# 15 of the 31 taps of a convolution's second half move from VectorE to GpSimd

## The chip, the cores and the metric

The kernel runs on one core of a Trainium2 chip. The metric is the device time of one launch in microseconds (us). The engines are called as in the profile: PE is TensorE, DVE is VectorE, ACT is ScalarE, POOL is GpSimd, SP is SyncE. An instruction is named by its line in the kernel, as L436.

## The reference, cut to what matters

One decoder layer works on 512 prompt tokens and 8 x 4 sample tokens, 1024 features wide. Its token mixer has three branches on the same input; the third is a convolution module: a gated product, a causal depthwise convolution of width 31 over 256 channels, a layer norm, a swish and a matrix.

```python
glu = c_in[..., :W_CONV] * jax.nn.sigmoid(c_in[..., W_CONV:])
cc, new_conv = _dwconv(glu, conv_buf, conv_dw, conv_b)
br_c = jax.nn.silu(_layernorm(cc, conv_ln_g, conv_ln_b)) @ conv_pw
merged = gates[:, :, 0] * br_a + gates[:, :, 1] * br_b + gates[:, :, 2] * br_c
```

`_dwconv` gives, for each channel and token t, the sum over j from 0 to 30 of weight[j] times glu[t - 30 + j], plus a bias. All is in 32-bit floats.

## The kernel before, in words

Features lie on the 128 partitions, tokens along the columns, so the 256 channels of the convolution are two blocks c = 0 and 1 of 128 partitions. `ge[c]` holds the gated product of a block with its 30 tokens of history, `acc[c]` the convolved result: 32 sample columns, then 512 prompt columns.

The matrix products are made by `gemm` (L228), each from three passes over operands split into a high and a low part. The high part of a weight chunk is written by ACT (L133), the rest by DVE (L134); the chunk can be used when both are there.

The convolution is in `conv_work`, a generator. For the sample tokens POOL forms products (L425, 128x248) and DVE sums them (L426, L427). For the prompt tokens DVE does one tap after the other: the first is a multiplication with the bias added (L434), each further one is L436, which multiplies a shifted view of `ge[c]` by a column of weights and adds `acc[c]`, on 128x512. The two blocks alternate. That makes two L434 and 60 L436. With `NV1 = 31` the branch that would use ACT and POOL for block 1 is never taken. `conv_norm` then transposes `acc` on PE (L457), normalises it and makes the operands that the sample stage multiplies much later.

Which instruction stands where in an engine's queue is not the order of the code. A planner lays the queues out by its own estimate of durations, following data dependences and giving preference to what comes earlier in the code. On the chip each queue then runs in that order. The code reaches the convolution (`pump(100)`) after the first attention unit, yet its taps stand in the DVE queue from 44 us on, between other work: the weight parts L134, the gate products L499, the parts of queries and keys L218 and L215, and L515. L515 scales the products of the pooling branch out of the "z" buffer in PSUM; there is one such buffer (a pair of banks), and the next product into it (L511, later L581) needs it empty. Half of these read-outs are done by ACT (L517), half by DVE (L515), eight each.

POOL's queue in this stage holds copies of state (L357, L384, L401, L405), the products L425, and the issue of a few DMAs (L385, L386, L406, L407); later it copies keys (L546) and issues the gathers of the cache.

Of the kernel before, what the change touches and what calls it, by code (L numbers as in the profile page):

```python
# [9 lines left out]
F32 = mybir.dt.float32  # L10
# [3 lines left out]
ALU = mybir.AluOpType  # L14
PSUM = bass.MemoryType.PSUM

P = 128
D = 1024
KD = D // P
NP = 512  # L20
DB = 8
DS = 4
NS = DB * DS
T = NP + NS
# [7 lines left out]
CW = 31  # L32
# [15 lines left out]
V_BG, V_PS, V_CB, V_CG, V_CLB, V_G1, V_B1, V_DW, V_SB, V_SR = 0, 24, 32, 34, 36, 38, 46, 54, 116, 124  # L48
# [5 lines left out]
NGA = 2  # L54
NGB = 3
PUMP = 4
NV1 = 31
GACT = 3
VACT = False
CNU = 0  # L60
# [88 lines left out]
def hybrid_layer_kernel(  # L149
# [6 lines left out]
    nc = tc.nc  # L156
# [79 lines left out]
    def vcol(c):  # L236
        return vt[:, c:c + 1]

    def sview(ap, s):
        return ap.rearrange("p (b s) -> p b s", s=s)  # L240
# [32 lines left out]
    cvp = conv_st.enter_context(pool("cvp"))  # L273
    GEW = CB + NP + DB * CEXT
    ge = [cvp.tile([P, GEW], F32, tag="ge", bufs=2, name=f"ge{c}") for c in range(2)]
    acc = [cvp.tile([P, T], F32, name=f"acc{c}") for c in range(2)]
# [76 lines left out]
    for c in range(2):  # L353
# [11 lines left out]
        for lev in range(2 if c == 0 else 4):  # L365
            sh = 1 << lev
            a0 = 2 * sh - 1
            o = s1.tile([P, n], F32, tag=f"sum{lev}", name=f"sum{c}{lev}")
# [5 lines left out]
        for s in range(2):  # L374
            r = slice(64 * s, 64 * s + 64)
            nc.vector.scalar_tensor_tensor(out=pf[r, NS + PB:], in0=sm[s][r, 2 * PB:PB + NP], scalar=ec_(E_IW + c, 1)[r],
                                           in1=ue[r, 2 * PB:PB + NP], op0=ALU.mult, op1=ALU.subtract)
            nc.vector.scalar_tensor_tensor(out=sview(pf[r, :NS], DS), in0=sview(sm[s][r, PB + NP:], PEXT)[:, :, PB:], scalar=ec_(E_IW + c, 1)[r],
                                           in1=uv[r, :, PB:], op0=ALU.mult, op1=ALU.subtract)
# [38 lines left out]
    def conv_work():  # L418
        for c in range(2):
            gv = sview(ge[c][:, CB + NP:], CEXT)  # L420
            dw = vt[:, V_DW + c * CW:V_DW + (c + 1) * CW].unsqueeze(1).to_broadcast([P, DB, CW])
            pr = cvp.tile([P, DS, DB, CW], F32, tag="prs", name=f"prs{c}")
            av_ = sview(acc[c][:, :NS], DS)
            for s in range(DS):
                nc.gpsimd.tensor_tensor(out=pr[:, s], in0=gv[:, :, s:s + CW], in1=dw, op=ALU.mult)  # L425
            nc.vector.reduce_sum(av_.rearrange("p b s -> p s b"), pr, axis=mybir.AxisListType.X)  # L426
            nc.vector.tensor_scalar(acc[c][:, :NS], acc[c][:, :NS], vcol(V_CB + c), None, op0=ALU.add)  # L427
            yield
        for j in range(CW):
            for c in range(2):  # L430
                dw = vcol(V_DW + c * CW + j)
                o, v = acc[c][:, NS:], ge[c][:, j:j + NP]
                if j == 0:
                    nc.vector.tensor_scalar(o, v, dw, vcol(V_CB + c), op0=ALU.mult, op1=ALU.add)  # L434
                elif c == 0 or j < NV1:
                    nc.vector.scalar_tensor_tensor(out=o, in0=v, scalar=dw, in1=o, op0=ALU.mult, op1=ALU.add)  # L436
                else:
                    pr = cvp.tile([P, NP], F32, tag="pr", bufs=2, name=f"pr{j}", padded_shape=[P, T])
                    nc.scalar.mul(pr, v, dw)
                    nc.gpsimd.tensor_tensor(out=o, in0=pr, in1=o, op=ALU.add)  # L440
            yield

    def conv_norm():
        rows = (P, P, P, P, NS)
# [29 lines left out]
        return last  # L474

    cw = conv_work()

    def pump(n):
# [615 lines left out]
    for m in range(KD):  # L1094
# [10 lines left out]
        for (c0, c1), ps in zip(HALVES, pss):  # L1105
            v = xf[:, m, c0:c1]
# [183 lines left out]
```

## Time and profile before

| | |
|---|---|
| time, median of 3 runs | 866.68 us (865.34 to 867.08) |
| time of the profiled execution | 872.77 us |
| its span | 871.0 us |
| PE busy | 827.4 us (95%), 6683 instructions |
| DVE busy | 580.5 us (67%), 968 instructions |
| ACT busy | 413.4 us (47%), 711 instructions |
| POOL busy | 174.1 us (20%), 198 instructions |
| mean granted TensorE clock | 0.975 |

The busy shares are means over stages that differ: the page's picture of the span in 40 slices has DVE at 8 or 9 tenths from the second to the fifth slice, 22 to 109 us, and at 4 to 6 tenths in many others. An instruction's duration includes time in which it is held up after its start; neighbouring instructions on DVE overlap by a little (a fill of some 0.07 us), so their number over the time they take together gives a somewhat smaller figure than their mean duration. The releaser in brackets is the instruction that ended the idle time before a row, as the profile infers it.

### The profile page before, as it was taken

The numbers are of one execution on the slowest core, as the hardware profiler recorded it, in microseconds if no ns is written. First come the engines' busy times: TensorE is split into PE (matmuls) and PEld (weight loads), VectorE is DVE, ScalarE is ACT, GpSimd is POOL, SyncE is SP. The second block draws the span as 40 slices with busy tenths as digits, with TensorE's granted clock in tenths as the row PEclk, the third lists the DMA queues.
The fourth block names the chain that finished last, engine by engine and source line by source line (L and its number), as shares of the span: only waits on it lengthen the run. The fifth ranks groups of instructions, "written<-read, shape, count | busy, mean of one in ns | idle before, by whom it ended". The sixth has DMA issues, their size and how long they took to land.

```text
span 871.0 us, 16214 instructions
## 1 busy us (share of the span) xinstructions
PE 827.4 (95%) x6683; PEld 779.1 (89%) x6683; DVE 580.5 (67%) x968; ACT 413.4 (47%) x711; POOL 174.1 (20%) x198
## 2 busy tenths in 40 slices
PE   8998899999999998999998699999999999999992
PEld 7998799888898786789997699999999999999992
DVE  4899956888555544469455999883337888843436
ACT  5334368677654324344316556553124555543231
POOL 1430000002547766210000032211000111110002
PEclk9999899999999998999999699999999999999997
DMA  9413132412738987673500153322225333312222
GB/s 297 125 48 106 55 93 62 147 40 87 266 119 289 341 320 259 216 272 116 146 2 1 48 145 99 97 68 82 85 83 146 98 98 100 108 55 83 74 93 103
DMA packets 119401, 110.35 MB, mean 127 GB/s; under 512 B 4896, under 2 KB 111232, under 8 KB 117152
## 3 DMA queue, kind: packets, MB, share of 16 engines
q1 hardware_dynamic: 110848, 73.12, 28.2%
q0 software_dynamic: 8480, 36.20, 11.9%
q8 instruction: 52, 0.85, 0.4%
q14 instruction: 21, 0.17, 0.1%
HBM read 104.44 MB, written 4.87 MB: 125 GB/s over the span
## 4 chain that ended last, share of the span: by engine, by line
PE 81%; DVE 8%; DMA 5%; issue 2%; ACT 2%; POOL 1%; SPq 0%; DVEq 0%; POOLq 0%; ACTq 0%
PE mm L228 73%; DVE acc L436 3%; DMA raw<-in_w_in 2%; PE z L581 1%; PE o L607 1%; DVE wl L134 1%; PE tp L602 1%; PE z L677 1%; PE o L704 1%; PE tp L819 1%; DMA vr<-in_cv,piv 1%; DMA kr<-in_ck,pix 1%; DMA xt<-in_x_t 1%; ACT wh L133 0%; ACT xf L897 0%
## 5 line engine op out<-in xcount | busy, mean ns | idle before, releaser
L228 PE MATMUL mm<-xh,wh 128*128 128x256 f32 (+1 forms) x672 | 198.3, 295 | 3.0 <-DVE gt L492 0.9
L228 PE MATMUL mm<-xl,wh 128*128 128x256 f32 (+1 forms) x672 | 196.8, 293 | 0.5 <-DVE xl L215 0.4
L228 PE MATMUL mm<-xh,wl 128*128 128x288 f32 (+1 forms) x672 | 196.4, 293 | 0.4 <-DVE wl L134 0.4
L133 ACT CAST wh<-raw 128x1024 fp32r<-128x1024 f32 (+2 forms) x93 | 84.8, 915 | 164.0 <-PE mm L228 142.8
L134 DVE TENSOR_TENSOR wl<-raw,wh 128x1024 fp32r<-128x1024 f32 (+2 forms) x93 | 100.1, 1079 | 71.5 <-ACT wh L133 70.9
L228 PEld LDWEIGHTS mm<-xh,wh 128*128 128x128 f32 x672 | 128.0, 191 | 9.2 <-issue 3.8
L228 PEld LDWEIGHTS mm<-xl,wh 128*128 128x128 f32 x672 | 127.8, 190 | 4.5 <-issue 3.1
L228 PEld LDWEIGHTS mm<-xh,wl 128*128 128x128 f32 x672 | 127.8, 191 | 3.5 <-issue 2.4
L228 PE MATMUL mm<-gh,wh 128*128 128x288 f32 (+1 forms) x352 | 101.6, 290 | 0.0
L228 PE MATMUL mm<-gh,wl 128*128 128x288 f32 (+1 forms) x352 | 101.3, 288 | 0.0
L228 PE MATMUL mm<-gl,wh 128*128 128x288 f32 (+1 forms) x352 | 100.8, 287 | 0.0
L644 POOL DMA_INDIRECT kr<-in_ck,pix x64 | 67.0, 1047 | 36.1 <-issue 14.8
L228 PEld LDWEIGHTS mm<-gl,wh 128*128 128x128 f32 x352 | 66.4, 189 | 0.0
L228 PEld LDWEIGHTS mm<-gh,wl 128*128 128x128 f32 x352 | 66.2, 188 | 0.0
L228 PEld LDWEIGHTS mm<-gh,wh 128*128 128x128 f32 x352 | 65.9, 188 | 0.1
L978 POOL TENSOR_TENSOR gl<-g,gh 128x272 fp32r<-128x272 f32 x22 | 26.2, 1193 | 194.1 <-ACT gh L977 191.7
L978 POOL TENSOR_TENSOR gl<-sg,gh 128x272 fp32r<-128x272 f32 x22 | 19.7, 894 | 140.3 <-ACT gh L977 140.3
L436 DVE SCALAR_TENSOR_TENSOR acc<-ge,vt,acc 128x512 f32<-128x512 f32 x60 | 42.6, 752 | 0.1
L228 PE MATMUL mm<-mh,wh 128*128 128x256 f32 (+1 forms) x128 | 37.7, 294 | 0.0
L228 PE MATMUL mm<-ml,wh 128*128 128x256 f32 (+1 forms) x128 | 37.5, 293 | 0.0
L228 PE MATMUL mm<-mh,wl 128*128 128x256 f32 (+1 forms) x128 | 37.1, 290 | 0.0
L913 DVE TENSOR_TENSOR wl<-rawf,wh 128x1024 fp32r<-128x1024 f32 x22 | 28.3, 1287 | 8.8 <-ACT wh L912 8.7
(292 smaller groups left out, 2170.7 us busy)
## 6 DMA issues: line engine op xcount, KB each, us to landing
raw<-in_w_in SPq DMA_DIRECT2D x14, 1024.0 KB, 6.3
rawf<-in_w_g SPq DMA_DIRECT2D x22, 512.0 KB, 4.1
rawf<-in_w_u SPq DMA_DIRECT2D x22, 512.0 KB, 5.4
raw<-in_w_in SPq DMA_DIRECT2D x12, 512.0 KB, 3.8
raw<-in_w_d SPq DMA_DIRECT2D x16, 384.0 KB, 3.4
raw<-in_w_d SPq DMA_DIRECT2D x16, 320.0 KB, 3.2
raw<-in_w_out SPq DMA_DIRECT2D x4, 1024.0 KB, 5.4
raw<-in_w_att_o SPq DMA_DIRECT2D x4, 512.0 KB, 3.7
```

Of the source, the lines that this page charges most:

```text
L133: self.nc.scalar.copy(hi[:, a:b], v[:, a:b])
L134: self.nc.vector.tensor_tensor(out=lo[:, a:b], in0=v[:, a:b], in1=hi[:, a:b].bitcast(F32), op=ALU.subtract)
L228: ins = nc.tensor.matmul(ps[:, :n], lw, rr, start=first and s == 0, stop=last and s == len(steps) - 1, **kw)
L436: nc.vector.scalar_tensor_tensor(out=o, in0=v, scalar=dw, in1=o, op0=ALU.mult, op1=ALU.add)
L581: nc.tensor.matmul(zps[s][:, :wd], a[r, qs], b[r, :wd], start=n_ == 0, stop=n_ == 2)
L602: nc.tensor.transpose(tp[:, kb], rc[:, s, kb * P:(kb + 1) * P], ident)
L607: nc.tensor.matmul(op_[64 * s:64 * s + 64, :P], vtok[:, kb, 64 * s:64 * s + 64], ats[s][:, kb], start=kb == 0, stop=kb == i)
L644: nc.gpsimd.indirect_dma_start(out=kr[:, u].rearrange("p h c -> p (h c)"), out_offset=None, in_=ck, in_offset=bass.IndirectOffsetOnAxis(ap ...
L677: behind["z"] = nc.tensor.matmul(zp[32 * jj:32 * jj + 32, :256], qbd[:, hp, b], kvt[b, "k", jj][:, :, hp], start=hp == 0, stop=hp == 3)
L704: nc.tensor.matmul(op_[32 * c:32 * c + 32], at[:, j], kvt[b, "v", j // 4][:, j % 4], start=j >= 4, stop=False)
L913: nc.vector.tensor_tensor(out=l, in0=src, in1=h.bitcast(F32), op=ALU.subtract)
L978: nc.gpsimd.tensor_tensor(out=gl[:, f % NFC, c0:c0 + TH], in0=g, in1=gh[:, f % NFC, c0:c0 + TH].bitcast(F32), op=ALU.subtract)
```

## The change

`NV1` becomes 16: of block 1, DVE does taps 0 to 15. The other 15 are done by POOL in a tile of its own, `part`: the first is a multiplication by the weight column, each of the 14 others a multiplication into a second tile `pr` and an addition of that to `part`. These 29 instructions stand in the code ahead of the taps of DVE. Behind the last tap DVE adds `part` to `acc[1]`. Block 0 stays as it was: 31 taps on DVE. Both new tiles use the tag `pr`, whose two buffers `conv_norm` uses later for the swish.

```diff
-NV1 = 31
+NV1 = 16
...
+        part = cvp.tile([P, NP], F32, tag="pr", bufs=2, name="part", padded_shape=[P, T])
+        pr = cvp.tile([P, NP], F32, tag="pr", bufs=2, name="prod", padded_shape=[P, T])
+        for j in range(NV1, CW):
+            v, dw = ge[1][:, j:j + NP], vcol(V_DW + CW + j)
+            if j == NV1:
+                nc.gpsimd.tensor_scalar(part, v, dw, None, op0=ALU.mult)
+            else:
+                nc.gpsimd.tensor_scalar(pr, v, dw, None, op0=ALU.mult)
+                nc.gpsimd.tensor_tensor(out=part, in0=part, in1=pr, op=ALU.add)
         for j in range(CW):
             for c in range(2):
                 dw = vcol(V_DW + c * CW + j)
...
                 elif c == 0 or j < NV1:
                     nc.vector.scalar_tensor_tensor(out=o, in0=v, scalar=dw, in1=o, op0=ALU.mult, op1=ALU.add)
-                else:
-                    pr = cvp.tile([P, NP], F32, tag="pr", bufs=2, name=f"pr{j}", padded_shape=[P, T])
-                    nc.scalar.mul(pr, v, dw)
-                    nc.gpsimd.tensor_tensor(out=o, in0=pr, in1=o, op=ALU.add)
             yield
+        nc.vector.tensor_tensor(out=acc[1][:, NS:], in0=acc[1][:, NS:], in1=part, op=ALU.add)
+        yield
```

## Rows read from the trace of the kernel before

**Rows 1.** The page's chain that ended last, by engine and by line.
```profile
PE 81%; DVE 8%; DMA 5%; issue 2%; ACT 2%; POOL 1%; SPq 0%; DVEq 0%; POOLq 0%; ACTq 0%
PE mm L228 73%; DVE acc L436 3%; DMA raw<-in_w_in 2%; PE z L581 1%; PE o L607 1%; DVE wl L134 1%; PE tp L602 1%; PE z L677 1%; PE o L704 1%; PE tp L819 1%; DMA vr<-in_cv,piv 1%; DMA kr<-in_ck,pix 1%; DMA xt<-in_x_t 1%; ACT wh L133 0%; ACT xf L897 0%
```

**Rows 2.** Busy time by stretch: stretch, length, engines (instructions), granted clock, DMA.
```profile
core 0: us, PE busy (x) PEld busy (x) DVE busy (x) ACT busy (x) POOL busy (x), PEclk, DMA share, GB/s
51.05:73.22 22.17, 21.11 (x170) 19.75 (x169) 22.17 (x34) 8.28 (x14) 0.17 (x1) 1.00 0.22 64
73.22:91.02 17.80, 12.26 (x101) 11.39 (x100) 17.80 (x28) 8.08 (x12) 0.00 (x0) 0.98 0.30 89
91.02:109.37 18.35, 18.16 (x125) 17.69 (x126) 17.17 (x30) 6.26 (x15) 1.98 (x4) 0.84 0.23 72
109.37:220.00 110.63, 110.63 (x910) 99.58 (x909) 83.91 (x160) 83.91 (x165) 11.64 (x18) 1.00 0.28 85
...
91.68:96.97 5.29, 5.29 (x25) 5.29 (x25) 5.29 (x10) 0.40 (x1) 0.21 (x1) 0.50 0.00 0
```

**Rows 3.** PE's timeline: start, length, instruction, idle time before it and its releaser.
```profile
70.07 0.40 PE L511 MATMUL z<-ph,wh 64*128 64x288 f32 x2 [0.49 <-DVE mg L515]
...
86.09 0.39 PE L511 MATMUL z<-ph,wh 64*128 64x256 f32 x2 [1.23 <-DVE mg L515]
...
91.02 0.47 PE L581 MATMUL z<-kh,qh 64*128 64x128 f32 x2 [4.31 <-DVE mg L515]
```

**Rows 4.** One line's instructions: count, shortest/median/longest ns, first and last start.
```profile
L515 DVE TENSOR_SCALAR mg<-z,vt x8: 470/488/505, 50.6 to 90.4; 128x288 f32<-128x288 f32 x4, 128x256 f32<-128x256 f32 x4
...
L436 DVE SCALAR_TENSOR_TENSOR acc<-ge,vt,acc x60: 731/739/1168, 44.3 to 108.3; 128x512 f32<-128x512 f32 x60
L457 PEld LDWEIGHTS tp<-et,acc x10: 94/141/142, 123.4 to 130.9; 128*128 128x128 f32 x8, 128*32 128x32 f32 x2
...
L402 DVE TENSOR_TENSOR ge<-av,sg x2: 679/922/1164, 41.9 to 48.5; 128x512 f32<-128x512 f32 x2
```

**Rows 5.** DVE's timeline, beside POOL's work and without it.
```profile
26.34 0.85 DVE L376 SCALAR_TENSOR_TENSOR pf<-sum,et,ue 64x497 f32<-64x497 f32 x1
...
27.60 0.74 DVE L376 SCALAR_TENSOR_TENSOR pf<-sum,et,ue 64x497 f32<-64x497 f32 x1
...
45.85 1.05 DVE L436 SCALAR_TENSOR_TENSOR acc<-ge,vt,acc 128x512 f32<-128x512 f32 x1
46.83 1.70 DVE L134 TENSOR_TENSOR wl<-raw,wh 128x1024 fp32r<-128x1024 f32 x1
...
49.54 1.17 DVE L436 SCALAR_TENSOR_TENSOR acc<-ge,vt,acc 128x512 f32<-128x512 f32 x1
...
55.40 1.21 DVE L134 TENSOR_TENSOR wl<-raw,wh 128x1024 fp32r<-128x1024 f32 x1
...
92.45 6.04 DVE L436 SCALAR_TENSOR_TENSOR acc<-ge,vt,acc 128x512 f32<-128x512 f32 x9
...
549.60 1.76 DVE L913 TENSOR_TENSOR el<-rawf,eh 128x1024 fp32r<-128x1024 f32 x1
...
569.08 1.23 DVE L913 TENSOR_TENSOR el<-rawf,eh 128x1024 fp32r<-128x1024 f32 x1 [0.16 <-ACT eh L912]
```

**Rows 6.** POOL's timeline: its copies and its additions and products.
```profile
25.62 1.82 POOL L401 COPY ge<-scs 128x240 f32<-128x240 f32 x2
...
37.38 0.39 POOL L405 COPY fm<-ge 128x240 f32<-128x240 f32 x1 [6.91 <-DVE ge L403]
...
38.90 0.69 POOL L425 TENSOR_TENSOR prs<-ge,vt 128x248 f32<-128x248 f32 x1
...
45.23 4.92 POOL L425 TENSOR_TENSOR prs<-ge,vt 128x248 f32<-128x248 f32 x4
...
93.07 0.21 POOL L546 COPY ksf<-kf 128x32 f32<-128x32 f32 x1 [41.85 <-ACT kf L545]
...
302.94 2.67 POOL L750 TENSOR_TENSOR mg<-mg,gt 128x544 f32<-128x544 f32 x2
...
549.50 0.77 POOL L978 TENSOR_TENSOR gl<-g,gh 128x272 fp32r<-128x272 f32 x1 [3.51 <-ACT gh L977]
```

## The prediction

> **What bounds the kernel now.** I read the chain of waits first, since it says which engine ends last: PE carries 81% of it, and the largest piece that isn't a TensorE instruction is the convolution tap of VectorE (DVE), 3% of the span [rows 1]. So the kernel is a TensorE kernel, and this change can move the time only where PE waits for DVE. The busy time by stretch shows that place [rows 2]. From 51.05 to 91.02 DVE is busy without a gap, and PE loses 1.06 us of the first 22.17 and 5.54 of the next 17.80. Then it runs for 5.29 us at a granted clock of 0.50, the lower of its two levels, and loses half of that, 2.6. Together some 9 us: that is all this stage has to give. From 91.02 on PE is hardly ever idle (18.16 of 18.35, then 110.63 of 110.63).
>
> PE's own timeline says what it waited for [rows 3]: each time L515, a DVE instruction that empties the one "z" buffer; the last wait is 4.31 us and ends at 91.02. L515 is late because the DVE queue, which runs strictly in order, has taps in front of it. The eighth and last L515 starts at 90.4 [rows 4]; the long row of nine taps begins at 92.45, after it [rows 5].
>
> **The change part by part.**
>
> *15 taps leave DVE.* An L436 alone takes 0.74 us [rows 4] and occupies 0.67 of the queue (nine in 6.04 us) [rows 5], so 15 x 0.67 = 10.0 us of DVE work go. Which 15? Before, 60 L436 and two L434 (j = 0) stand in the queue; after, 45 and two. 17 of the 60 start after 91.0: one at 91.13, the nine of 92.45 and seven more up to 108.3; 43 stand ahead. If the order is kept, the missing 15 are the last ones, from 93.1 on, behind the L515 that holds PE. PE runs almost without idling there, and the result isn't used until the transposes of L457 at 123.4 [rows 2, 4]. So the saving is worth nothing to PE: the lateness that it feels at 91.02 comes from the 43 taps that stay. Were a removed tap ahead of it, it would be worth 0.67 us.
>
> *One addition comes to DVE.* 128x512 with two inputs in SBUF; the like L402 took 0.68 us at its shortest [rows 4]. It stands behind the last tap, near 93 of the old order, and the time to the transposes covers it. Its wait for GpSimd (POOL) would hold the DVE queue, so POOL's end is worked out below.
>
> *29 instructions come to POOL.* 15 multiplications by a column and 14 additions, all 128x512, from about 51.2, when POOL has issued its last DMA of this part. POOL then sits idle for 41.85 us, up to the copy L546 at 93.07 [rows 6], so their own length is covered. What isn't covered is what they do to DVE. From 45.23 POOL ran four L425 back to back, with DVE beside it. An L425 alone is 0.69; these four took 4.92, so 1.23 each [rows 6]. The DVE instructions beside them grew as well: L436 from 0.74 to 1.05 and 1.17, L134 from 1.21 to 1.70, L402 from 0.68 to 1.16 [rows 4, 5], that is by 0.31, 0.43, 0.49 and 0.48, mean 0.43. In the FFN an L913 with an L978 (128x272, 0.77) beside it took 1.76 instead of 1.23: 0.53 more [rows 5, 6]. The two engines take turns, one DVE instruction to one of POOL, and DVE pays POOL's lone duration less some 0.25 us.
>
> Price of an addition: alone 0.69 us at 248 columns and 1.33 at 544 (2.67 for two) [rows 6], so 1.26 at 512, and DVE pays 1.0. 14 x 1.0 = 14.0 us.
>
> Price of a multiplication: the trace has none on POOL. The nearest with one input are copies: 0.21 us at 32 columns, 0.39 at 240 [rows 6], so about 0.63 at 512. Beside the copies of 240 columns from 25.62 an L376 took 0.85 instead of 0.74 [rows 5, 6], 0.11 more, which is the lone duration less 0.28. At 512 that is 0.35 each. Lower end: the copy's 0.11 unchanged; upper end: the price of an addition, 1.0. I take 0.35, as a multiplication by a column reads one tile, like the copy: 15 x 0.35 = 5.3 us (1.7 to 15). Below nothing it can't go, as no DVE row beside POOL is shorter than alone.
>
> From this goes what falls beside DVE instructions that read PSUM or only one tile (L426 and three L515 in the stretch): there POOL gets ahead at no cost, by about 2.5 of the 29, 1.7 us. Sum: 14.0 + 5.3 - 1.7 = 17.6 us.
>
> The page "SBUF — State Buffer" of the Trainium skill, section "Who interferes with whom", says that a VectorE instruction with two SBUF inputs and a GpSimd instruction that reads SBUF exclude each other, and that the loser blocks until the other has finished. The taking of turns agrees with it; by its letter DVE would pay POOL's whole duration, which the 0.43 of 0.69 does not bear out.
>
> *Where the 17.6 us end up.* Each POOL instruction lets one DVE instruction pass; the 29th contended DVE instruction after 51.05 stands near 74 of the old order. So POOL is done at about 51 + 23 + 17.6 = 92 us, and the whole delay is laid on DVE before the L515 of 90.4, for which PE already waits without slack. DVE reaches it at 108, and PE goes on at 108.6 instead of 91.02. The final addition, near 111, finds POOL done 19 us earlier and waits for nothing; POOL's L546 waits for PE's products and comes as late as PE. Eight L515 from 50.6 to 90.4 are 5.7 us apart [rows 4]; while POOL runs they stand 10 to 11 apart, so PE can run even at its lower level between them and not be later, except behind the last wait, as now. After that PE is busy without a gap for 110 us [rows 2], so nothing gives the delay back, and the later loads follow PE.
>
> The profiled execution took 872.77 us (span 871.0, 1.8 around it). With 17.6 it would take 890.4. It lies 6.1 over the median of the runs, 866.68; the same step on that gives 884.3.
>
> **The rivals.**
>
> *A: the price is higher.* Multiplications at 1.0 us make the sum 14 + 15 less 2: 27 us, 894. DVE paying POOL's lone durations in full makes it 14 x 1.26 + 15 x 0.63 less 2.3: 25 us, 892. A low clock behind three new waits, not hidden, adds 3 x 2.6 to the forecast: 892. For it: the rows have no POOL multiplication, and the clock fell behind one wait of 4.31 us [rows 2, 3]. Against it: 0.43 of 0.69, and PE's room between two L515.
>
> *B, on the other side: the queue is laid out anew.* The DVE order is made by a planner, which has 15 taps fewer to place and may put L515 and the weight splits L134 ahead of more taps. Place: the eighth L515. Price: each tap that moves behind it takes 0.67 us off PE's wait. At 17.6 / 0.67 = 26 taps of 43 it comes out even; if nearly all go, the 9 us lost today come back: 858. For it: the convolution has slack until 123.4. Against it: the 43 taps need no removed tap's place, and today's order lets PE wait 4.31 us behind taps that have slack.
>
> The page "Perfetto Trace Analysis" of the Trainium skill, section "Optimizing Scalar/DVE Operations", allows that giving work of a saturated VectorE away can pay, and warns that between VectorE and GpSimd it might not help. The grown DVE rows agree with the warning.
>
> *C: a wash.* The order moves by about as many taps as POOL costs: within 1.7 us of 866.7.
>
> *D: POOL becomes the bound.* If a multiplication took 2.5 us or more of POOL's time, the final addition would wait past 111 and hold what stands behind it on DVE: 895 or above. No one-input row is near that.
>
> **How the numbers follow.** Forecast 0.62 (its own range 880 to 890), A and D together 0.16, B 0.15, C 0.07. About 0.2%, 1.7 us, is what a measurement of this kernel tells from no change. Faster 0.15, same 0.07, slower 0.78. The range for 8 in 10 leaves out the better half of B and the end of A and D: 862 to 897.
>
> **What would show it.** In the profile after: DVE busy from 51 to about 108 without a gap; an L436 of 1.5 to 1.8 us while POOL adds and about 1.1 while it multiplies, 0.74 again when POOL is done; POOL busy from 51 to about 92; PE's last wait for L515 ending near 108; no wait of the last addition for POOL. Wrong would be: L436 at 0.74 beside POOL (the price fails), or PE's waits for L515 gone while L436 grew (the order changed, B), or DVE idle before its last addition (D).

## The result, and the profile after

The changed kernel takes 880.97 us (median of 4 runs, 879.1 to 881.97), the kernel before 866.01 on the same chip: a ratio of 1.0169 (95% interval 1.0147 to 1.0192). That is 14.6 us slower by the ratio and 15.0 by the medians. The forecast was 884.3, within 862 to 897. The profiled execution took 879.1 us, its span is 877.1.

Lines from 434 on have moved: the tap is now L445, the read-out of "z" L522, the products behind it L518 and L588; POOL's multiplications are L434 and L436, its additions L437, the last addition on DVE L447. Busy time in the stretches of [rows 2], with the same columns:

```profile
51.05:73.22 22.17, 18.48 (x135) 17.14 (x134) 22.17 (x23) 6.73 (x10) 21.26 (x12) 0.94 0.11 33
73.22:91.02 17.80, 12.56 (x85) 11.68 (x85) 17.80 (x18) 5.94 (x9) 16.89 (x11) 0.79 0.10 30
91.02:109.37 18.35, 9.73 (x65) 8.80 (x64) 18.17 (x24) 4.57 (x10) 7.71 (x6) 0.77 0.27 87
109.37:220.00 110.63, 110.63 (x897) 101.39 (x897) 78.82 (x149) 78.31 (x156) 12.40 (x17) 0.99 0.26 78
```

DVE is full in the first two stretches, as before, and now in the third as well (18.17 of 18.35), but it gets through 23 instructions in the first instead of 34. PE idles 3.69, 5.24 and 8.62 us, where it idled 1.06, 5.54 and 0.19. The waits of PE between 30 and 180 us name the place again (sum, times, longest), with the product that waits last in the timeline:

```profile
PE z L518 <- DVE mg L522: 12.3, 5, 5.0
PE z L588 <- DVE mg L522: 3.1, 1, 3.1
PE mm L228 <- DVE wl L134: 1.1, 1, 1.1
```
```profile
104.64 0.47 PE L588 MATMUL z<-kh,qh 64*128 64x128 f32 x2 [3.10 <-DVE mg L522]
```

This product came at 91.02 [rows 3]; it is 13.6 us late. The first product with the new keys, near the end of the attention stage, has moved from 222.0 (first line, the kernel before) to 236.3:

```profile
L662 PE MATMUL z<-qbd,ksf x8: 379/379/403, 222.0 to 223.5; 128*32 128x256 f32 x8
```
```profile
L669 PE MATMUL z<-qbd,ksf x8: 379/379/403, 236.3 to 237.8; 128*32 128x256 f32 x8
```

That start is the mark by which I compare all runs below: it is read from one profiled execution each, and it leaves out the sample stage. There the profiled executions differ for a reason of their own. In the kernel before, one DMA of weights (`raw<-in_w_in`) stood in the chain of waits for 20.35 us from 309.9; in the changed kernel no DMA of 10 us or more does. From the first cache product to the first transpose of the output projection the profiled execution of before took 167.0 us, the changed one 159.7. So the two profiled spans are only 6.1 us apart, the medians 15.0, and the mark 14.3: medians and mark agree.

DVE beside POOL, from the two timelines (start, length, instruction):

```profile
57.26 1.21 DVE L134 TENSOR_TENSOR wl<-raw,wh 128x1024 fp32r<-128x1024 f32 x1
58.39 1.76 DVE L445 SCALAR_TENSOR_TENSOR acc<-ge,vt,acc 128x512 f32<-128x512 f32 x1
...
60.47 6.61 DVE L445 SCALAR_TENSOR_TENSOR acc<-ge,vt,acc 128x512 f32<-128x512 f32 x6
...
106.06 4.50 DVE L445 SCALAR_TENSOR_TENSOR acc<-ge,vt,acc 128x512 f32<-128x512 f32 x4
...
116.61 0.69 DVE L447 TENSOR_TENSOR acc<-acc,part 128x512 f32<-128x512 f32 x1 [2.69 <-POOL part L437]
```
```profile
55.79 1.88 POOL L436 TENSOR_SCALAR prod<-ge,vt 128x512 f32<-128x512 f32 x1
57.75 1.86 POOL L437 TENSOR_TENSOR part<-part,prod 128x512 f32<-128x512 f32 x1
...
93.85 2.47 POOL L436 TENSOR_SCALAR prod<-ge,vt 128x512 f32<-128x512 f32 x1
106.68 0.21 POOL L553 COPY ksf<-kf 128x32 f32<-128x32 f32 x1 [10.36 <-ACT kf L552]
106.85 1.27 POOL L437 TENSOR_TENSOR part<-part,prod 128x512 f32<-128x512 f32 x1
...
111.80 1.57 POOL L436 TENSOR_SCALAR prod<-ge,vt 128x512 f32<-128x512 f32 x1
114.62 0.62 POOL L554 DMA_DIRECT2D out<-kf  x1 [1.26 <-ACT kf L552]
115.26 1.31 POOL L437 TENSOR_TENSOR part<-part,prod 128x512 f32<-128x512 f32 x1
```

A tap that meets an addition takes 1.76 instead of 0.74; six taps take 6.61 instead of 4.0. POOL's chain isn't done at 92 but at 116.6, since a multiplication takes 1.57 us or more, and since the key copy stands in the middle of the chain in POOL's queue: from 96.3 on POOL waits 10.36 us for that copy's input. The last addition then holds DVE for 2.69 us.

### The profile page after: what moved, and what is told of

Same layout as the page of the kernel before. It is cut to its first block, busy times and chain, and to the rows that moved or that the text cites. A ratio compares the mean times of both kernels' runs of the same rounds, so it can differ in the third digit from the quotient of the medians.

```text
span 877.1 us, 16229 instructions
## 1 busy us (share of the span) xinstructions
PE 827.5 (94%) x6683; PEld 778.7 (89%) x6683; DVE 588.1 (67%) x954; ACT 413.5 (47%) x711; POOL 228.4 (26%) x227
## 4 chain that ended last, share of the span: by engine, by line
PE 84%; DVE 9%; issue 2%; ACT 2%; DMA 2%; POOL 0%; SPq 0%; DVEq 0%; ACTq 0%
PE mm L228 75%; DVE acc L445 4%; PE z L684 2%; PE o L711 1%; PE z L588 1%; PE o L614 1%; DVE wl L134 1%; PE tp L609 1%; PE tp L826 1%; DMA vr<-in_cv,piv 1%; DMA xt<-in_x_t 1%; DVE mg L506 1%; ACT xf L904 0%; DVE mg L522 0%; PE o L714 0%
## 5 line engine op out<-in xcount | busy, mean ns | idle before, releaser
L134 DVE TENSOR_TENSOR wl<-raw,wh 128x1024 fp32r<-128x1024 f32 (+2 forms) x93 | 99.7, 1075 | 72.1 <-ACT wh L133 71.4
L985 POOL TENSOR_TENSOR gl<-sg,gh 128x272 fp32r<-128x272 f32 x22 | 21.5, 979 | 134.4 <-ACT gh L984 134.4
L445 DVE SCALAR_TENSOR_TENSOR acc<-ge,vt,acc 128x512 f32<-128x512 f32 x45 | 47.1, 1078 | 0.3
```

The costliest lines, as they stand in the source:

```text
L134: self.nc.vector.tensor_tensor(out=lo[:, a:b], in0=v[:, a:b], in1=hi[:, a:b].bitcast(F32), op=ALU.subtract)
L985: nc.gpsimd.tensor_tensor(out=gl[:, f % NFC, c0:c0 + TH], in0=g, in1=gh[:, f % NFC, c0:c0 + TH].bitcast(F32), op=ALU.subtract)
```

## The experiments

The runs stand on four chips, on which the kernel before takes 866, 882, 866 and 884 us, so each run is told by its ratio to the kernel before on its own chip, and by the mark (222.0 before, from the first chip alone). In nearly all runs the same 1657 matmuls of PE, give or take one, stand ahead of the mark; in e7_hold12 there are 1683 and in e10_hold4_late_norm 1700, so there the mark comes later in PE's work. The expectations count their own theories: theory 1 is the prediction's mechanism, and rivals 1 to 5 are explained where they first appear.

| run | ratio (95% interval) | in us | mark | against 222.0 |
|---|---|---|---|---|
| the change | 1.0169 (1.0147 to 1.0192) | +14.6 | 236.3 | +14.3 |
| e1_no_pool | 1.0024 (1.0004 to 1.0045) | +2.1 | 220.7 | -1.3 |
| e2_extra_pool | 1.0207 (1.0164 to 1.0250) | +18.3 | 238.2 | +16.2 |
| e3_mult_only | 1.0073 (1.0025 to 1.0120) | +6.4 | 226.9 | +4.9 |
| e4_add_only | 1.0165 (1.0114 to 1.0216) | +14.6 | 232.6 | +10.6 |
| e5_memset | 1.0307 (1.0289 to 1.0326) | +26.6 | 245.9 | +23.9 |
| e5b_fill_late | 0.9984 (0.9957 to 1.0011) | -1.4 | 221.5 | -0.5 |
| e6_late_pool | 1.0162 (1.0128 to 1.0197) | +14.0 | 234.8 | +12.8 |
| e7_hold12 | 1.0181 (1.0159 to 1.0203) | +15.7 | 224.3 | +2.3 |
| e7_hold4 | 1.0089 (1.0069 to 1.0110) | +7.7 | 226.7 | +4.7 |
| e10_hold4_late_norm | 1.0031 (1.0011 to 1.0052) | +2.7 | 221.4 | -0.6 |
| e8_act_readout | 0.9866 (0.9831 to 0.9901) | -11.8 | 212.7 | -9.3 |
| e9_after_act | 1.0053 (1.0026 to 1.0081) | +4.7 | 226.5 | +4.5 |

**e1_no_pool: the taps leave, POOL does nothing.** Against the changed kernel:

```diff
-            if j == NV1:
-                nc.gpsimd.tensor_scalar(part, v, dw, None, op0=ALU.mult)
-            else:
-                nc.gpsimd.tensor_scalar(pr, v, dw, None, op0=ALU.mult)
-                nc.gpsimd.tensor_tensor(out=part, in0=part, in1=pr, op=ALU.add)
...
-        nc.vector.tensor_tensor(out=acc[1][:, NS:], in0=acc[1][:, NS:], in1=part, op=ALU.add)
```

> The changed kernel without POOL's 29 instructions and without the last addition (taps 15 to 30 of block 1's second part, 15 of 31, are left out of the sum): 47 taps on DVE and nothing beside them. Theory 1 (POOL's instructions make DVE's longer ahead of the L515 that holds PE): about 864, that is 2 us under before, since 40 instead of 43 taps stand ahead of the last L515, and the other removed taps are worth nothing. Rival 1 (the loss comes from the new order of DVE's queue): about 881, as the changed kernel, since the order up to there is the same. Rival 2 (DVE's fullness is the cost, each tap taken off is worth its 0.67 us up to the 9 us that PE loses): 857.

The mark came 1.3 us early and the whole time 2.1 us late. Ten us of DVE work are gone, and 1.3 are won at the mark: rival 2 falls, and as the 14.3 are missing, so does rival 1. DVE's last tap starts at 93.7 instead of 108.3, but PE's waits are nearly the old ones:

```profile
PE z L577 <- DVE mg L511: 3.2, 1, 3.2
PE z L507 <- DVE mg L511: 1.9, 2, 1.1
```

The whole time is 3.4 us worse than the mark. The profile shows a loss right behind the mark: a stretch with 102 matmuls that takes 12.80 us in the kernel before (first line) takes 17.40 here, at a granted clock of 0.80 instead of 1.00.

```profile
227.90:240.70 12.80, 11.14 (x102) 10.32 (x101) 8.44 (x16) 6.14 (x11) 4.11 (x5) 1.00 0.67 258
```
```profile
226.60:244.00 17.40, 14.31 (x102) 12.85 (x101) 8.50 (x16) 6.19 (x11) 4.14 (x5) 0.80 0.50 190
```

Whether the kernel before loses that on this chip too is not on record, so this part stays open.

**e2_extra_pool: POOL works, no tap leaves.**

```diff
-NV1 = 16
+NV1 = 31
+NP1 = 16
...
-        for j in range(NV1, CW):
+        for j in range(NP1, CW):
...
-            if j == NV1:
+            if j == NP1:
...
-        nc.vector.tensor_tensor(out=acc[1][:, NS:], in0=acc[1][:, NS:], in1=part, op=ALU.add)
```

> The kernel before, all 62 taps on DVE, with POOL's 29 instructions added and their sum used by nothing (no last addition). Theory 1: before + 16, about 882, the 24 or so POOL instructions ahead of the last L515 at 1.0 us for an addition and 0.4 for a multiplication. Rival 3 (the last addition's wait for POOL, 2.7 us in the changed kernel, and what stands behind it makes the loss): 866, as before, since there is no last addition. Rival 1 (order): 866, since the taps stand as before.

POOL's 29 instructions run as in the change, from tap NP1 on. The mark moved by 16.2, the figure expected, and the total by 18.3. The loss is POOL's presence beside DVE, not the order of the queue nor the last addition, which isn't there: rivals 1 and 3 fall. With 43 taps ahead of the last read-out it is 1.9 us worse than the change, which has 40: 3 x 0.67 = 2.0.

**e3_mult_only and e4_add_only: one kind each.** First the edit of the run with 15 multiplications, then that of the run with 14 additions, whose loop stands in place of the other.

```diff
-                nc.gpsimd.tensor_tensor(out=part, in0=part, in1=pr, op=ALU.add)
```
```diff
+        for j in range(NV1 + 1, CW):
+            v = ge[1][:, j:j + NP]
+            nc.gpsimd.tensor_tensor(out=part, in0=ge[1][:, NV1:NV1 + NP] if j == NV1 + 1 else part, in1=v, op=ALU.add)
```

> The changed kernel with POOL's 15 multiplications and without its 14 additions (14 taps are left out of the sum). A multiplication took 1.57 to 1.88 us on POOL in the changed kernel, an addition 1.4. Theory 1 with the price by what the DVE instruction beside it grew by (0.35 to 0.4 each): 15 x 0.4 less 4 taps x 0.67 = +3.3, about 869. Rival 4 (DVE pays by POOL's busy time, 15 x 1.7 = 26 us of the 50): about half of the loss or more, 874 to 878.

> The changed kernel with 14 POOL additions of unweighted views and without the multiplications (the second part of block 1's sum is without its weights). Theory 1 with 1.0 us each: 14 less 4 taps x 0.67 = +11.3, about 877. Rival 4 (by POOL's busy time, 14 x 1.4 = 20 us of 50): +4 to +6, 870 to 872.

Both have 39 taps ahead of the last read-out, one less than e1. From e1's -1.3, then, the multiplications cost 4.9 + 1.3 + 0.7 = 6.9 us, 0.46 each, and the additions 10.6 + 1.3 + 0.7 = 12.6, 0.90 each. Rival 4 falls by e4, whose mark and total both lie far above its 4 to 6 us: on POOL the multiplications were the longer ones (2.2 us against 1.6), on DVE they cost half as much. By e3 alone it would not: there the total, +6.4, lies above the 3.3 of theory 1, with an interval that reaches into rival 4's figures. The timelines show why a multiplication costs less, first POOL and DVE of the run with multiplications, then those with additions:

```profile
52.93 31.34 POOL L436 TENSOR_SCALAR prod<-ge,vt 128x512 f32<-128x512 f32 x14
```
```profile
56.74 1.21 DVE L134 TENSOR_TENSOR wl<-raw,wh 128x1024 fp32r<-128x1024 f32 x1
57.88 1.18 DVE L444 SCALAR_TENSOR_TENSOR acc<-ge,vt,acc 128x512 f32<-128x512 f32 x1
...
59.37 4.84 DVE L444 SCALAR_TENSOR_TENSOR acc<-ge,vt,acc 128x512 f32<-128x512 f32 x6
```
```profile
52.31 21.10 POOL L432 TENSOR_TENSOR part<-part,ge 128x512 f32<-128x512 f32 x13
```
```profile
61.14 1.75 DVE L440 SCALAR_TENSOR_TENSOR acc<-ge,vt,acc 128x512 f32<-128x512 f32 x1
...
63.21 9.25 DVE L440 SCALAR_TENSOR_TENSOR acc<-ge,vt,acc 128x512 f32<-128x512 f32 x6
72.38 2.11 DVE L134 TENSOR_TENSOR wl<-raw,wh 128x1024 fp32r<-128x1024 f32 x1
```

Beside additions every DVE instruction grows, by 0.87 on the mean of six taps and by 0.90 at L134: strict turns. A multiplication of 2.2 us lets two or three DVE instructions pass and lengthens one of them, by 0.35 to 0.44; the L134 here isn't touched.

**e5_memset and e5b_fill_late: POOL writes only.** Both put fills in place of the 29 instructions, 58 in the first run and 59 in the second. The first starts them behind the last L425 (`prs_`), the second behind a copy that needs the first tap of block 1.

```diff
+        with tc.issue_after(prs_.ins):
+            for j in range(2 * (CW - NV1)):
+                nc.gpsimd.memset(part, 0.0)
+                if j > 1:
+                    nc.gpsimd.memset(pr, 0.0)
```
```diff
+                        ins = nc.gpsimd.tensor_copy(tiny, acc[1][:, NS - 1:NS + 1])
+                        with tc.issue_after(ins.ins):
+                            for i in range(59):
+                                nc.gpsimd.memset(pr if i % 2 else part, 0.0)
```

> The changed kernel with POOL's 29 instructions replaced by 59 fills of 128x512, which write SBUF and read nothing (the second part of block 1's sum is zero). POOL is about as busy from 50 us on. Theory 1 in the form 'two engines that read SBUF take turns': DVE's taps beside the fills stay at 0.74 us, the first attention product O<-at starts within 2 us of 119.2, as without POOL, and the time is within 3 us of that run's ratio (1.002). Rival 5 (any work of POOL slows DVE, by the occupied engine or its queue): taps of 1.0 us and more, first attention product at 127 or later, 8 us or more over before.

> The changed kernel with POOL's 29 instructions replaced by 59 fills of 128x512 that only write, started when the first tap of block 1 is done (the second part of block 1's sum is left out), so that between 52 and 80 us DVE runs taps, weight splits and gate products with two SBUF inputs beside them. Theory 1 in the form 'two engines that read SBUF take turns': taps stay at 0.74 us, first attention product within 2 us of 119.2. Rival 5 (any POOL work slows any DVE work): taps longer, first attention product later by 5 us or more.

The first run went against both theories: the mark came 23.9 us late, and one instruction did it, the first tap of block 1, which multiplies one SBUF tile into another:

```profile
51.76 26.03 DVE L441 TENSOR_SCALAR acc<-ge,vt 128x512 f32<-128x512 f32 x1
77.71 0.73 DVE L443 SCALAR_TENSOR_TENSOR acc<-ge,vt,acc 128x512 f32<-128x512 f32 x1
```

It takes 0.53 alone. The fills ran from 49.71 to 78.25, one every 0.47 us. The tap began among the first of them, at 51.76, and ended at 77.79, during the last one: between back-to-back fills it got no turn. With that one instruction out of the way, POOL's fills, 30 of `part` and 29 of `pr`, cost nothing, and taps, L134 and L505 beside them keep their lengths:

```profile
L442 POOL MEMSET part<- x30: 515/520/525, 53.6 to 80.7; 128x512 f32 x30
```
```profile
57.21 4.06 DVE L444 SCALAR_TENSOR_TENSOR acc<-ge,vt,acc 128x512 f32<-128x512 f32 x6
61.18 1.23 DVE L134 TENSOR_TENSOR wl<-raw,wh 128x1024 fp32r<-128x1024 f32 x1
```

So what takes turns is reading, for DVE instructions with two SBUF inputs; rival 5 falls for them and stands for the one-input instruction. The Trainium skill, "SBUF — State Buffer", section "Who interferes with whom", states both: a VectorE instruction with two SBUF inputs contends with a GpSimd instruction that reads SBUF, not with one that only writes it, and a `tensor_scalar` can enter a 2-port mode, which contends with GpSimd. The two runs agree: 4.06 us for six taps beside fills, 26.03 for the `tensor_scalar`.

**e6_late_pool: POOL's chain after the last read-out.**

```diff
+        with tc.issue_after(ksi[0].ins):
+            for j in range(NV1, CW):
```

`ksi[0]` is the first key copy on POOL.

> The changed kernel with POOL's 29 instructions queued behind its first key copy, so from about 92 us on, after the last L515, where PE is busy without a gap and DVE is not full. Nothing is left out. Theory 1: the price is still paid by DVE but no longer by PE at the z buffer; first attention product at 119 to 122 instead of 134.8, taps few beside POOL; total within -2 to +5 us of before, as DVE's other work of the attention stage grows by up to 16 us spread over 50. Rival 4 (POOL's total work is what counts, wherever it stands): +14 as the changed kernel.

The first attention product stood where it had been before the change, at 120.5, but the mark came 12.8 us late: the loss only moved. The convolution's result is late now, and PE's queue holds the transposes of its normalisation (L478) ahead of other work:

```profile
PE tp L478 <- DVE cna L472: 2.4, 1, 2.4
PE tp L478 <- ACT cf L479: 1.9, 1, 1.9
```
```profile
150.00:170.00 20.00, 15.53 (x114) 14.04 (x112) 10.55 (x33) 8.48 (x16) 2.44 (x4) 0.95 0.48 146
170.00:190.00 20.00, 17.71 (x122) 13.79 (x123) 15.08 (x28) 16.56 (x36) 1.27 (x2) 0.80 0.05 15
```

PE idles 6.8 us in these two stretches, where in the kernel before it was never idle, at a granted clock of 1.00. Here 20 us at 0.95 and 20 at 0.80 are some 5 us more, by an estimate from these rows, so the two stretches hold nearly all of the 12.8. The total, +14.0, is the figure of rival 4, but not by its cause: POOL's work beside DVE moved nothing up to 120.5. So my expectation failed: I had taken the attention stage for slack, since DVE isn't full there.

**e7_hold12, e7_hold4, e10_hold4_late_norm: before, with taps held behind the last read-out.**

```diff
+                    with tc.issue_after(mgl[0].ins) if j >= 12 else ExitStack():
                         nc.vector.scalar_tensor_tensor(out=o, in0=v, scalar=dw, in1=o, op0=ALU.mult, op1=ALU.add)
...
-CNU = 0
+CNU = 4
```

`mgl[0]` is the last L515; the bound is 12 in e7_hold12 and 4 in the two others, and `CNU` is changed in e10 alone.

> The kernel before, with the taps of j = 12 and up (38 of 62) held behind the last L515 in DVE's queue; 22 instead of 43 L436 stand ahead of it. No POOL taps, nothing is left out. Theory 1 (PE loses its 9 us because taps stand ahead of L515, not because DVE has too many taps): the waits for L515 go, first attention product 5 to 9 us earlier than 120.5, total -4 to -9 us. Rival 2 (DVE is simply full, the number of taps counts): no change, the wait moves behind the last L515.

> As e7_hold12, with the taps of j = 4 and up (54 of 62) held behind the last L515; 6 stand ahead. Theory 1: waits for L515 gone as well, but 36 us of taps now stand in the attention stage; first attention product 4 to 9 us earlier, total -2 to -8 us. Rival 2: 0 to +10, as the attention stage fills up.

> The kernel before with the taps of j = 4 and up held behind the last L515, as in the run that held 54 taps, and the normalisation of the convolution (its transposes on PE) placed after the fifth attention unit instead of the first. Nothing is left out. In the run that held 54 taps the first attention product came at 113.0 instead of 120.5, and that was lost again where PE's queue waited for the late normalisation (4.2 us, then a lower clock). If that is so: the first attention product stays near 113 and PE has no wait of over 1 us for the normalisation; total -4 to -8 against before. If DVE's taps in the attention stage are themselves the cost: 0 to +5.

With 22 taps ahead of the last read-out, one wait of 2.8 us for it is left. With 6 ahead PE's waits for it are gone and the first query product comes at 84.9 instead of 91.0, but in e7_hold4 the gain is lost in the attention stage: PE waits for the normalisation, and its clock falls.

```profile
PE tp L471 <- DVE cna L465: 4.2, 1, 4.2
```
```profile
150.00:170.00 20.00, 12.78 (x73) 9.68 (x73) 14.27 (x39) 11.37 (x21) 0.00 (x0) 0.69 0.25 81
```

With the normalisation placed later (e10) that wait is gone. The mark, 0.6 us early, hides how far this carries, since more matmuls stand ahead of it than before. Up to 222.0 us PE has done 1703 in e10 (second line) and 1658 in the kernel before:

```profile
0.00:222.00 222.00, 211.94 (x1658) 195.16 (x1658) 178.98 (x308) 131.81 (x247) 34.98 (x57) 0.98 0.35 107
```
```profile
0.00:222.00 222.00, 215.66 (x1703) 199.02 (x1704) 177.94 (x304) 134.32 (x246) 34.55 (x56) 1.00 0.36 110
```

The kernel before has done 1700 matmuls at 227.9, e10 at 221.4, some 6 us sooner. So there the taps that were held back did find a place in the attention stage. Behind the mark the gain is gone:

```profile
221.40:241.90 20.50, 14.28 (x101) 11.66 (x102) 11.44 (x21) 10.37 (x19) 11.35 (x11) 0.83 0.68 225
```

The kernel before takes 12.80 us for as many matmuls (shown at e1). e1 takes 17.40 there without this edit, so not all of the loss is put down to it. The totals that theory 1 expected were wrong in all three runs; where e10 loses its gain is shown, why is open. e7_hold12 is odd: 2.3 at the mark, 15.7 in the end. Its chain has a DMA of weights of 19.66 us in the sample stage (from 315.84), like the profiled execution of before; why it falls there in some executions and not in others stays open.

**e8_act_readout and e9_after_act: the read-out leaves the queue of taps.** Before, and the changed kernel, with one edit:

```diff
-                    if s:
-                        nc.vector.tensor_scalar(mg[:, mo, c0:c1], pss[s][:, :c1 - c0], vcol(V_PS + mo), None, op0=ALU.mult)
-                    else:
-                        nc.scalar.mul(mg[:, mo, c0:c1], pss[s][:, :c1 - c0], vcol(V_PS + mo))
+                    nc.scalar.mul(mg[:, mo, c0:c1], pss[s][:, :c1 - c0], vcol(V_PS + mo))
```

> The kernel before, with all 16 read-outs of the z buffer on ACT (the eight L515 leave DVE); all 62 taps on DVE, order otherwise the planner's. Nothing is left out. Theory 1 (PE loses its time at the z buffer because L515 stands behind taps): PE's waits for a read-out go, the first attention product comes 5 to 9 us before 120.5, and the total is 4 to 9 us under before, since the end of the taps and the normalisation stay where they were. Rival 2 (DVE full): the wait passes to the weight splits L134 or to the query and key parts behind the same taps; 0 to -3.

> The changed kernel with the same step: read-outs on ACT, POOL's 29 instructions as changed. Theory 1: DVE is still some 16 us late by the time POOL has done its work, but PE meets that only at the weight splits, which are prepared two chunks ahead; first attention product at 124 to 130 instead of 134.8, total +4 to +10 over before. If the z buffer were the only way in which DVE's lateness reaches PE: first attention product at 112 to 116, total -4 to -8. If every DVE instruction in that queue holds PE alike: 134, +14.

On the kernel before, PE runs without a gap and without a fall of the clock from 51 to 109, with all 62 taps on DVE:

```profile
51.05:73.22 22.17, 22.17 (x178) 20.64 (x178) 22.17 (x33) 11.85 (x22) 0.41 (x1) 1.00 0.16 47
73.22:91.02 17.80, 17.80 (x146) 17.34 (x144) 17.26 (x27) 9.57 (x17) 0.97 (x1) 1.00 0.41 117
91.02:109.37 18.35, 18.35 (x152) 18.00 (x151) 16.55 (x28) 8.85 (x19) 1.86 (x3) 1.00 0.39 117
```

The mark moves by -9.3, the 9 us that the stage had to give, and the total by -11.8, more than expected. This version is faster than both kernels. (The planner laid PE's queue out anew as well: 658 matmuls instead of 610 stand ahead of the first query product.)

```profile
L659 PE MATMUL z<-qbd,ksf x8: 379/379/403, 212.7 to 214.2; 128*32 128x256 f32 x8
```
```profile
L666 PE MATMUL z<-qbd,ksf x8: 379/379/403, 226.5 to 228.1; 128*32 128x256 f32 x8
```

On the changed kernel (second line) the same edit takes the mark from +14.3 to +4.5. POOL's loss now reaches PE by the other road, the weight splits and the query parts in the same queue:

```profile
PE mm L228 <- DVE wl L134: 6.4, 2, 3.7
PE mm L228 <- DVE ql L218: 1.2, 1, 1.2
```

The figures that theory 1 gave for e9 came out, but they were counted from the kernel before. With the read-outs on ACT the kernel to compare with is e8, on the same chip: against it POOL's taps cost 13.8 us at the mark (226.5 against 212.7) and 14.1 by the medians (887.84 against 873.77), as much as with the read-outs on DVE. The last of the three expectations, that every DVE instruction in that queue holds PE alike, fits this better: the first attention product comes at 124.8, 13.6 us behind that of e8 (111.2). Moving the read-outs wins back what PE lost before the change, and spares nothing of what POOL costs.

## Why the prediction was right, step by step

- *Where PE waits.* Right. The waits are for the same read-out, with the ends moved, and e8 shows it by itself: take the read-out out of that queue and the 9 us come back. But the read-out is not the only way to PE: e9 against e8 loses 13.8 us with no read-out on DVE.
- *The 15 taps are worth nothing to PE.* Right in substance (e1: -1.3 at the mark). The count was off by three: 40 taps stand ahead of the last read-out, not 43. From tap 16 on only block 0's taps are left, and the planner puts fewer of them between the other work. That is 2.0 us on the good side.
- *Price of an addition, 1.0.* Measured 0.90 (e4), and 1.02 on single taps in the change.
- *Price of a multiplication, 0.35.* Measured 0.46 (e3). The reason I gave (one tile read costs DVE less) fits; its basis doesn't: the copies led me to 0.63 us on POOL, and it takes 1.57 to 2.9. What DVE pays isn't POOL's duration less a constant: even 1.57 less 0.25 would be 1.3. That 0.35 came so near is luck.
- *The sum.* 24 of the 29 instructions fell ahead of the last read-out: 13 x 0.46 + 11 x 0.90 less the 2.0 = 13.9, against 13.6 at the product behind that read-out and 14.3 at the mark. All 29 at the measured prices would be 15 x 0.46 + 14 x 0.90 = 19.5, so the forecast's 17.6 was 1.9 too low in its prices; the five instructions that came later (2 x 0.46 + 3 x 0.90 = 3.6) and the three taps (2.0) then took off more than that. The errors partly cancel, so the nearness of the number is in part luck.
- *POOL is done at 92.* Wrong by 25 us, in two steps. That each POOL instruction lets one DVE instruction pass holds for additions alone; a multiplication lets two or three pass (e3). And I had the key copy L546 come behind the chain, while the planner put it inside, so POOL waited 10.36 us for PE's products. The last addition did wait for POOL, 2.69 us. I had named that as a sign of being wrong (rival D), and for this step it was; but D's price, 895 or above, didn't follow: PE is busy without a gap from 109 on.
- *Nothing gives the delay back.* Right: 13.6 us at 104.6, 14.3 at 236.3, and 14.6 to 15.0 in the total.
- *The clock.* It fell in the new waits, as the granted clock of 0.79 and 0.77 shows. Behind the last wait it cost little that is new: from that product to the mark the kernel before takes 131.0 us (91.0 to 222.0) and the changed one 131.7. Ahead of it PE waits for DVE, and the sum closes within half a microsecond without a term for the clock.
- *Rival B* came only in small, as three taps fewer ahead of the read-out (2.0 us): PE's waits for the read-out stayed and the taps grew. Its slack "until 123.4" is a bound: e6 and e7_hold4 delayed the end of the convolution far past it, to 152.5 and 147.0, and PE paid in the normalisation. Clearing the order ahead of the last read-out (e10) won some 6 us over the first 1700 matmuls and nothing in the total.

## What to carry to other kernels

Work taken from a full engine is worth what stands ahead of the instruction that another engine waits for, and no more: find that instruction, count what is in front of it, and first see whether it can leave the queue (here eight read-outs moved to ScalarE gave 9 us at the mark, 15 taps moved to GpSimd lost 14). What slows every instruction of a full queue is not cured that way: the taps on GpSimd cost 14 us with the read-outs in the queue or out of it. Before GpSimd is given elementwise work beside a busy VectorE, price it by what the VectorE instruction next to the like of it grows by in the trace, and not by GpSimd's own time. That an engine is not full in a stage doesn't make its work there free to come late: another queue may need the result in order (e6). And a time read at one instruction compares two kernels only if the same work stands ahead of it.

## What the runs showed of the hardware that I had not expected

- Beside a busy VectorE in the changed kernel, a GpSimd multiplication of 128x512 floats by a column took 1.57 to 2.94 us, an addition of two tiles of that size 1.27 to 1.86: the instruction with one input is the longer one on GpSimd and the cheaper one for VectorE (0.46 against 0.90 us each, e3 and e4).
- A one-input VectorE multiplication from SBUF to SBUF, 0.53 us alone, was held for 26.03 us by back-to-back GpSimd fills of 0.53 to 0.69 us (e5_memset); two-input VectorE instructions beside such fills kept their lengths (e5b_fill_late: fills of 0.52 us, six taps in 4.06 us, L134 at 1.23).
